# A hybrid decoder layer on one core: the gate's first block in front of the pairs, the values of heads 2 and 3 in a pair

## The chip, the cores and the metric

The kernel runs on one core of a Trainium2 chip. The metric is the device time of one execution in microseconds (us), as the median of several runs. Times within the program are us from the start of the profiled execution's span.

## The reference

The layer runs attention and a gated linear recurrence side by side on the same normalised and modulated input, and merges them by sigmoid gates. D is 1024, the sequence 1024, attention has 8 heads of 64.

```python
h = rmsnorm(x, norm_g[l]) * (1.0 + scale[:, None]) + shift[:, None]
proj = h @ w_in[l]
q_a, k_a, v_a, z_a, q_b, f_b, i_b, z_b, g_a, g_b = jnp.split(proj, cuts, axis=-1)
o_a = dilated_attention(heads_a(q_a), heads_a(k_a), heads_a(v_a), rel_bias)
o_a = o_a.reshape(B, S, ATTN_WIDTH).astype(x.dtype) * jax.nn.silu(z_a)
o_b = hgrn2_recurrence(...)   # from q_b, f_b, i_b, then rmsnorm and silu(z_b)
y = jax.nn.sigmoid(g_a) * (o_a @ w_branch_a[l]) + jax.nn.sigmoid(g_b) * (o_b @ w_branch_b[l])
x = x + gate[:, None] * (y @ w_out[l])
```

The change concerns two columns of the one large product `h @ w_in`: the values `v_a` of heads 2 and 3 (128 columns from VA + 128) and the first 128 columns of attention's gate `g_a`. The first are needed by attention, from head 2 on; the second only after attention, when its output is projected.

## The kernel before

**The stream.** The product with `w_in` is cut into blocks of 128 columns, and these are worked off as a stream of steps that fills TensorE during attention and the recurrence. Each factor is split into a high and a low part, and a product is three matmuls (L241, L242, L243). Two blocks together make a *pair* (`add_pair`), which by Strassen's scheme needs 7 steps of 12 matmuls of 512 columns; its seven products use sums of the input's quarters (b11, t1, t2, b22, b21, t3, t4). A block alone is a *unit* (`add_unit`, two steps of 24 matmuls). Of the 64 blocks, three (queries, keys and values of heads 0 and 1) are made while the input is still being prepared; 61 are left, so one unit stands in front of all pairs.

**The order.** Queries and keys of heads 2 and 3, of 4 and 5, the values of heads 4 to 7, the last queries and keys, then attention's silu inputs `z`, the gate blocks `ga`, `gb`, and the recurrence's blocks. Attention calls the stream by amounts of work (`fill`), so that a count of steps, not their contents, sets where each lies. Before a head is loaded (`load_head`), the steps that it needs are drawn forward if they are not done.

**What follows a block.** `ev_raw` copies a result to a buffer (L396) and stores it (L401). `ev_v` copies it too, but has TensorE turn it later (L452, 4 transposes for each half of the sequence), casts it into a high part on ScalarE (L456), subtracts on VectorE for the low part (L226) and stores both to `vq_d` (L458), four stores for two heads. Inside a pair, ScalarE also keeps three of the products in buffers (L330), the first of them before the product on t2 may go on in the same bank, the third before that on t3.

**The buffers.** All these results lie in one pool of six tiles of 128x512, called `ct` (`ctp`, `CT = 6`). A tile is free again when its store has landed, or when TensorE has turned it. ScalarE and VectorE work strictly in the order of their instructions, so one that waits for a free `ct` holds all behind it. Stores and weight loads leave from SP's queue, in order too; attention's own loads (L903, L909, L914) leave from GpSimd's queue.

**Around the change.** Two weight loads (w_raw6 and w_raw7) stand in SP's queue behind the last sums of the input's quarters (L685, t4), since they use that memory. Attention's first scores begin in the middle of the first pair. GpSimd waits for the last cast of the values of heads 0 and 1 (L901) before it loads the second half of head 0.

Of the kernel before, what the change touches and what calls it, by code (L numbers as in the profile page):

```python
# [19 lines left out]
P = 128  # L20
# [159 lines left out]
def hybrid_layer(ctx: ExitStack, tc: tile.TileContext, x, w_ada, b_ada, w_in, w_branch_a, w_branch_b, w_out,  # L180
# [26 lines left out]
    X = {}  # L207
# [9 lines left out]
    ga_d, gb_d, ya_d, ob_d = d8("ga_d"), d8("gb_d"), d8("ya_d"), d8("ob_d", 16)  # L217
# [5 lines left out]
    w_in_k, wba_k, wbb_k = kp(w_in), kp(w_branch_a), kp(w_branch_b)  # L223

    def sub(out_, a, hi):
        nc.vector.tensor_tensor(out_, a, hi.bitcast(F32), ALU.subtract)  # L226
# [6 lines left out]
    def banks():  # L233
        order.append(order.pop(0))
        return order[-1]

    def bank(tag):
        return pools["m"].tile([P, 512], F32, name=tag)

    def mm3(ps, ah, al, bh, bl, start, stop, more=False):  # L240
        nc.tensor.matmul(ps, ah, bh, start=start, stop=False, skip_group_check=more)  # L241
        nc.tensor.matmul(ps, al, bh, start=False, stop=False, skip_group_check=more)  # L242
        nc.tensor.matmul(ps, ah, bl, start=False, stop=stop, skip_group_check=more)  # L243

    def split(src):
        hi = wpool.tile([P, 4, P], F32R, name="w_hi")
        lo = wpool.tile([P, 4, P], F32R, name="w_lo")
        nc.scalar.copy(hi, src)  # L248
        sub(lo, src, hi)
        return hi, lo  # L250
# [6 lines left out]
    def piece(src, col, kh):  # L257
        def load(n):
            raw = raw_tile(n)
            nc.sync.dma_start(raw, src[:, 4 * kh:4 * kh + 4, col:col + P])  # L260
            return raw
        return stream.piece(load)

    def ctile(dt=F32):
        return ctp.tile([P, 512], dt, name="ct")
# [84 lines left out]
    def add_unit(src, col, rhs, ev, key=None, n=2, pre=None, alloc=None):  # L350

        stream.catch_up()
        ids = [piece(src, col, kh) for kh in range(n)]
        b = {}

        def add_half(kh):
            def prep():
                if kh == 0 and pre:
                    pre()
                parts = split(stream.tiles[ids[kh]])  # L360
                stream.done(ids[kh])
                return parts

            def run(parts):
                hi, lo = parts
                for th in range(2):
                    if th not in b:
                        b[th] = alloc() if alloc else bank(banks())
                    for k in range(4):
                        xh, xl = rhs(kh, th, k)  # L370
                        mm3(b[th], hi[:, k], lo[:, k], xh, xl, kh == 0 and k == 0, kh == n - 1 and k == 3)
                        if k < 3:
                            yield
                    if kh == n - 1:
                        ev(b[th], th, True)
                    if th == 0:
                        yield
            stream.add(prep, run)
        for kh in range(n):
            add_half(kh)  # L380
        if key:
            stream.key(key)

    QA, KA, VA, ZA = 0, AW, 2 * AW, 3 * AW
    QB, FB, IB, ZB = 4 * AW, 4 * AW + D, 4 * AW + 2 * D, 4 * AW + 3 * D
    GA, GB = 4 * AW + 4 * D, 4 * AW + 5 * D


    def half_of(th):
        return slice(512 * th, 512 * th + 512)  # L390

    def as_ct(src, psum):
        if not psum:
            return src
        t = ctile()
        nc.scalar.copy(t, src)  # L396
        return t

    def ev_raw(dst):
        def ev(src, th, psum):  # L400
            nc.sync.dma_start(dst[:, half_of(th)], as_ct(src, psum))  # L401
        return ev

    def ev_silu(dst):
        def ev(src, th, psum):
            t = ctile()
            nc.scalar.activation(t, src, AF.Sigmoid)
            out_ = t if psum else src
            nc.vector.tensor_tensor(out_, src, t, ALU.mult)
            nc.sync.dma_start(dst[:, half_of(th)], out_)  # L410
        return ev
# [9 lines left out]
    def ev_split(n, scale):  # L421
        def ev(src, th, psum):
            hi = ctile(F32R)
            if scale == 1.0:
                nc.scalar.copy(hi, src)
            else:
                nc.scalar.mul(hi, src, scale)
            lo = ctile(F32R) if psum else src.bitcast(F32R)
            if scale == 1.0:
                sub(lo, src, hi)  # L430
            else:
                nc.vector.scalar_tensor_tensor(lo, src, scale, hi.bitcast(F32), ALU.mult, ALU.subtract)
            nc.sync.dma_start(qk_d[n][:, half_of(th)], hi.bitcast(F32))
            nc.sync.dma_start(qk_d[n + 1][:, half_of(th)], lo.bitcast(F32))
        return ev

    def ev_q(p):
        return ev_split(4 * p, E ** -0.5)

    def ev_k(p):  # L440
        return ev_split(4 * p + 2, 1.0)
# [3 lines left out]
    def ev_v(p, wait=2):  # L445
        def ev(src, th, psum):
            t = as_ct(src, psum)

            def turn():
                pt = pools["t"].tile([P, 4, P], F32, name="pt")  # L450
                for n in range(4):
                    nc.tensor.transpose(pt[:, n], t[:, n * P:(n + 1) * P], ident)  # L452
                for n in (0, 2):
                    vs = ctile(F32R).rearrange("p (a h e) -> p a h e", a=2, h=2)
                    got = pt[:, n:n + 2].rearrange("p a (h e) -> p a h e", h=2)
                    nc.scalar.copy(vs[:, :, :, 0:E], got)  # L456
                    sub(vs[:, :, :, E:P], got, vs[:, :, :, 0:E])
                    nc.sync.dma_start(vq_d[p][:, 4 * th + n:4 * th + n + 2], vs.bitcast(F32))  # L458
                    last_v[p] = vs
                turned["v", p] = turned.get(("v", p), 0) + 1  # L460
            stream.after(wait, turn)
        return ev
# [28 lines left out]
    NAMES = {(0, 0): "b11", (0, 1): "b12", (1, 0): "b21", (1, 1): "b22"}  # L491
    FIRST = ((QA, ev_q(0)), (KA, ev_k(0)), (VA, ev_v(0)))
    ids = [piece(w_in_k, col, kh) for kh in range(2) for col, _ in FIRST]
    add_unit(w_in_k, VA + P, lambda kh, th, k: [t[:, k] for t in X[NAMES[kh, th]]], ev_v(1, 3), "first")
    pair = lambda a, b, ea, eb, key=None, closing=False: add_pair(w_in_k, a, b, ea, eb, key, closing)

    def pair_fq(h):
# [3 lines left out]
        pair(IB + h * P, ZB + h * P, ev_i(h), ev_silu(zb_d[h]), f"h{h}", closing)  # L501

    for p in (1, 2, 3):
        pair(QA + p * P, KA + p * P, ev_q(p), ev_k(p), f"qk{p}")
        if p == 2:
            pair(VA + 2 * P, VA + 3 * P, ev_v(2), ev_v(3), "v2")
    for m in (0, 2):
        pair(ZA + m * P, ZA + m * P + P, ev_silu(z_d[m]), ev_silu(z_d[m + 1]))
    for m in (0, 2, 4, 6):
        pair(GA + m * P, GA + m * P + P, ev_raw(ga_d[m]), ev_raw(ga_d[m + 1]))  # L510
    pair(GB, GB + P, ev_raw(gb_d[0]), ev_raw(gb_d[1]))
    pair_iz(0)
# [359 lines left out]
    with ExitStack() as at:  # L872
# [98 lines left out]
        def begin(n):  # L971

            if n < len(items):
                h, j = items[n]
                rows[n] = []
                for i in (2 * j, 2 * j + 1):
                    rows[n].append(score(h, i))
                    if i == 1:
                        if h > 0:
                            load_half(h, 1)  # L980
                        load_value(h, 1)
                    if i == 7 and h + 1 < NH:
                        load_head(h + 1)
                    yield
# [8 lines left out]
        first = begin(0)  # L993
# [510 lines left out]
```

## Time and profile before

| | us |
|---|---|
| Runs before: median (lowest to highest) | 1120.68 (1118.89 to 1120.88) |
| The profiled execution, its own time | 1119.58 |
| Its span in the profile | 1117.7 |
| TensorE busy, weight loads | 1093.9, 905.0 |
| VectorE, ScalarE, GpSimd busy | 807.4, 554.9, 124.0 |
| Start and transition, to 125 us | first pair from 83, attention's first scores at 95 |
| Attention with the stream beside it | 125 to 470 |
| Recurrence, merge and output | 470 to the end |

PE is TensorE, PEld its weight loads, DVE VectorE, ACT ScalarE, POOL GpSimd, SP the engine that issues most transfers. A row of the timeline gives start, length, engine, line, operation, what it writes from what, and in brackets the idle time ahead of it and what ended it. Where an instruction waits for several things, the bracket names the one that came last by the profile. A matmul's length is longer than its distance to the next one, because matmuls overlap. "Granted clock" is the share of TensorE's full clock that the chip allowed.

### The profile page before, as it was taken

To read this page: it belongs to the slowest core of one execution; us is meant where nothing else is said; L and a number is where in the kernel's file an instruction comes from. 1 tells how busy PE (TensorE), PEld (TensorE's weight loads), DVE (VectorE), ACT (ScalarE), POOL (GpSimd) and SP (SyncE) were. 2 spreads that over 40 slices of the span, in tenths; PEclk is the share of its full clock that TensorE was granted. 3 is DMA by queue.
4 is the path that set the end of the run, shared out by engine and by line. 5 is a ranking of instruction groups with operands and counts; after the bars stand their busy time and mean duration, and the time that the engine had idled before them with its cause. 6 is when DMAs were issued, how large, how long until landed. Compare 5 with 4: busy or idle time off the path is not lost.

```text
span 1117.7 us, 21827 instructions
## 1 busy us (share of the span) xinstructions
PE 1093.9 (98%) x8302; PEld 905.0 (81%) x8302; DVE 807.4 (72%) x1607; ACT 554.9 (50%) x1144; POOL 124.0 (11%) x207
## 2 busy tenths in 40 slices
PE   8998999999999999999999999999999999999997
PEld 6687888888888888888887888878887888888886
DVE  5586988878777776854788898897977773769053
ACT  6564656687555555632455554555554443334021
POOL 1112202203203201100000000000010012000000
PEclk9999999999999999999999999999999999999999
DMA  9849567637636624856625354453534379854052
GB/s 311 265 126 244 170 180 189 175 104 179 161 102 169 156 73 148 268 164 211 225 86 180 104 191 129 137 165 92 188 124 154 130 263 351 267 187 138 13 189 75
DMA packets 161608, 189.54 MB, mean 170 GB/s; under 512 B 11440, under 2 KB 107824, under 8 KB 161504
## 3 DMA queue, kind: packets, MB, share of 16 engines
q1 hardware_dynamic: 140080, 153.95, 43.1%
q0 software_dynamic: 21024, 33.60, 12.3%
q8 instruction: 65, 1.06, 0.4%
q10 hardware_dynamic: 400, 0.61, 0.2%
q14 instruction: 39, 0.32, 0.1%
HBM read 129.36 MB, written 58.76 MB: 168 GB/s over the span
## 4 chain that ended last, share of the span: by engine, by line
PE 79%; DVE 8%; DMA 6%; issue 3%; ACT 2%; POOL 1%; DVEq 0%; POOLq 0%; SPq 0%; ACTq 0%
PE m L241 17%; PE m L243 16%; PE m L242 16%; PE po L959 3%; PE pt L944 3%; PE pq L241 3%; PE pq L243 2%; PE pq L242 2%; PE pp L1125 2%; DMA gbr<-gb_d 2%; DVE w_lo L226 2%; PE pss L927 1%; PE pss L926 1%; DMA ld<-in_w_ada_dram 1%; PE pou L1221 1%
## 5 line engine op out<-in xcount | busy, mean ns | idle before, releaser
L226 DVE TENSOR_TENSOR w_lo<-w_raw,w_hi 128x512 fp32r<-128x512 f32 x156 | 106.9, 687 | 59.4 <-ACT w_hi L248 59.0
L248 ACT CAST w_hi<-w_raw 128x512 fp32r<-128x512 f32 x146 | 90.5, 621 | 43.7 <-PE m L243 29.2
L248 ACT CAST w_hi<-w_s 128x512 fp32r<-128x512 f32 x90 | 55.9, 621 | 56.6 <-PE m L243 37.9
L330 ACT COPY ct<-m 128x512 f32<-128x512 f32 x90 | 52.7, 585 | 58.4 <-PE m L243 48.8
L277 DVE TENSOR_TENSOR ct<-m,ct 128x512 f32<-128x512 f32 x90 | 61.8, 687 | 23.9 <-PE m L243 23.6
L226 DVE TENSOR_TENSOR w_lo<-w_s,w_hi 128x512 fp32r<-128x512 f32 x90 | 61.8, 687 | 11.7 <-ACT w_hi L248 10.6
L932 ACT ACTIVATE s<-s,st 128x128 f32<-128x128 f32 (+3 forms) x64 | 49.8, 778 | 33.0 <-DVE st L929 33.0
L948 ACT CAST pth<-pt 128x512 fp32r<-128x512 f32 (+1 forms) x80 | 43.5, 544 | 34.0 <-PE pt L944 29.7
L1229 POOL TENSOR_TENSOR ssh<-ssh,halfh 128x4 f32<-128x4 f32 x16 | 19.5, 1216 | 332.9 <-DVE ssh L1228 332.8
L226 DVE TENSOR_TENSOR ptl<-pt,pth 128x512 fp32r<-128x512 f32 (+1 forms) x80 | 50.6, 632 | 7.4 <-ACT pth L948 6.6
L241 PE MATMUL m<-t3h,w_hi 128*128 128x512 f32 x120 | 49.5, 412 | 2.2 <-ACT w_hi L248 2.2
L241 PE MATMUL m<-b22h,w_hi 128*128 128x512 f32 x124 | 50.9, 410 | 0.0
L241 PE MATMUL m<-b11h,w_hi 128*128 128x512 f32 x124 | 50.9, 410 | 0.0
L241 PE MATMUL m<-b21h,w_hi 128*128 128x512 f32 x124 | 50.6, 408 | 0.0
L241 PE MATMUL m<-t4h,w_hi 128*128 128x512 f32 x120 | 49.5, 412 | 1.1 <-issue 0.5
L242 PE MATMUL m<-b22h,w_lo 128*128 128x512 f32 x124 | 48.6, 392 | 1.8 <-issue 1.8
L241 PE MATMUL m<-t2h,w_hi 128*128 128x512 f32 x120 | 49.2, 410 | 0.7 <-ACT ct L330 0.7
L241 PE MATMUL m<-t1h,w_hi 128*128 128x512 f32 x120 | 49.4, 412 | 0.3 <-DVE ct L277 0.3
L243 PE MATMUL m<-b21l,w_hi 128*128 128x512 f32 x124 | 48.6, 392 | 0.0
L242 PE MATMUL m<-b11h,w_lo 128*128 128x512 f32 x124 | 48.6, 392 | 0.0
L243 PE MATMUL m<-b11l,w_hi 128*128 128x512 f32 x124 | 48.6, 392 | 0.0
L243 PE MATMUL m<-b22l,w_hi 128*128 128x512 f32 x124 | 48.6, 392 | 0.0
(365 smaller groups left out, 3226.6 us busy)
## 6 DMA issues: line engine op xcount, KB each, us to landing
w_raw<-in_w_in_dram SPq DMA_DIRECT2D x128, 256.0 KB, 3.5
wa<-in_w_ada_dram SPq DMA_DIRECT2D x16, 512.0 KB, 9.2
qk_d<-ct SPq DMA_DIRECT2D x32, 256.0 KB, 3.1
k<-qk_d POOLq DMA_DIRECT2D x64, 128.0 KB, 5.2
toep<-toep_d POOLq DMA_DIRECT2D x16, 256.0 KB, 5.5
qp<-qk_d POOLq DMA_DIRECT2D x32, 128.0 KB, 5.1
vq_d<-ct SPq DMA_DIRECT2D x16, 256.0 KB, 3.9
vq<-vq_d POOLq DMA_DIRECT2D x16, 256.0 KB, 4.3
```

The source lines that it names most:

```text
L226: nc.vector.tensor_tensor(out_, a, hi.bitcast(F32), ALU.subtract)
L241: nc.tensor.matmul(ps, ah, bh, start=start, stop=False, skip_group_check=more)
L242: nc.tensor.matmul(ps, al, bh, start=False, stop=False, skip_group_check=more)
L243: nc.tensor.matmul(ps, ah, bl, start=False, stop=stop, skip_group_check=more)
L248: nc.scalar.copy(hi, src)
L277: nc.vector.tensor_tensor(out_, a, b_, op)
L330: nc.scalar.copy(c[name], b[which])
L932: nc.scalar.activation(s[:, :kw], s[:, :kw], AF.Exp, bias=prev, scale=-1.0, accum_out=st2[:, 2:3])
L944: nc.tensor.transpose(pt[:, c0:c0 + P], pn[b][:, kt * P:(kt + 1) * P], ident)
L948: nc.scalar.copy(pth[:, :w], pt[:, :w])
L959: nc.tensor.matmul(po[:, 256 - n:256], vq[kt // 4][:, kt % 4], src[:, c0:c0 + n], start=kt == 0 and a == 0, stop=kt == 2 * j + 1 and a == 1)
L1125: nc.tensor.matmul(to[:, 0], k_[:, o:o + 32], q_[:, o:o + 32], start=True, stop=True)
```

## The change

The unit in front of the pairs computes the first block of `ga` instead of the values of heads 2 and 3. Those values form a new pair with the second block of `ga`, which stands behind the first pair of queries and keys. The remaining gate blocks are three pairs instead of four. The number of units, pairs, steps and matmuls is the same.

```diff
-    add_unit(w_in_k, VA + P, lambda kh, th, k: [t[:, k] for t in X[NAMES[kh, th]]], ev_v(1, 3), "first")
+    add_unit(w_in_k, GA, lambda kh, th, k: [t[:, k] for t in X[NAMES[kh, th]]], ev_raw(ga_d[0]), "first")
...
     for p in (1, 2, 3):
+        if p == 2:
+            pair(VA + P, GA + P, ev_v(1), ev_raw(ga_d[1]), "v1")
         pair(QA + p * P, KA + p * P, ev_q(p), ev_k(p), f"qk{p}")
         if p == 2:
             pair(VA + 2 * P, VA + 3 * P, ev_v(2), ev_v(3), "v2")
     for m in (0, 2):
         pair(ZA + m * P, ZA + m * P + P, ev_silu(z_d[m]), ev_silu(z_d[m + 1]))
-    for m in (0, 2, 4, 6):
+    for m in (2, 4, 6):
         pair(GA + m * P, GA + m * P + P, ev_raw(ga_d[m]), ev_raw(ga_d[m + 1]))
```

Two lines are added, so lines behind 503 have numbers higher by two in the changed kernel.

TensorE's order is the same but for the transposes of heads 2 and 3: eight in one place, between the products on t1 and t2 of the first pair, become twice four within attention. Around them other engines' orders move.

**ScalarE at the first pair.** Names carry their buffer's number here, and each row ends with what it waits for (an engine, or with DMAHW the landing of a transfer of SP's queue; eight such counters are used in turn). Before:

```order
L396 COPY ct_835<-m0_790 128x512 [waits DMAHW7_49,PE_49,Activation_49]
L396 COPY ct_849<-m1_803 128x512 [waits DMAHW0_49,PE_49,Activation_49]
L456 CAST ct_856<-pt_851 128x4x64 [waits DMAHW1_49,PE_49]
L456 CAST ct_860<-pt_851 128x4x64 [waits DMAHW4_49,DMAHW2_49,DVE_49]
L456 CAST ct_869<-pt_864 128x4x64 [waits PE_49,Activation_49]
L456 CAST ct_873<-pt_864 128x4x64 [waits DVE_49]
L248 CAST w_hi_878<-w_s_816 128x512 [waits DVE_49]
L330 COPY ct_895<-m2_882 128x512 [waits DMAHW5_49,PE_49,Activation_49]
```

In the changed kernel:

```order
L396 COPY ct_835<-m0_790 128x512 [waits DMAHW7_49,PE_49,Activation_49]
L396 COPY ct_850<-m1_803 128x512 [waits DMAHW0_49,PE_49,Activation_49]
L456 CAST ct_858<-pt_853 128x4x64 [waits DMAHW1_49,PE_49]
L456 CAST ct_862<-pt_853 128x4x64 [waits DMAHW4_49,DMAHW2_49,DVE_49]
L456 CAST ct_871<-pt_866 128x4x64 [waits DMAHW5_49,PE_49,Activation_49]
L456 CAST ct_875<-pt_866 128x4x64 [waits DVE_49]
L248 CAST w_hi_880<-w_s_816 128x512 [waits DVE_49]
L330 COPY ct_897<-m2_884 128x512 [waits PE_49]
```

The wait for the landing DMAHW5 has moved from the copy of the first product (ct_895) to the third cast of heads 0 and 1 (ct_871). The four casts of heads 2 and 3 that stood some rows further on are no longer here.

**SP's queue at the same place.** Before:

```order
L260 DMA w_raw7_976<-in_w_in_dram 128x4x128 [waits DMAHW4_49]
L458 DMA vq_d_97<-ct_856 128x512 [waits DMAHW5_49,DVE_49]
L458 DMA vq_d_97<-ct_860 128x512 [waits DMAHW6_49,DVE_49]
L458 DMA vq_d_97<-ct_869 128x512 [waits DMAHW7_49,DVE_49]
L458 DMA vq_d_97<-ct_873 128x512 [waits DMAHW0_49,DVE_49]
L458 DMA vq_d_97<-ct_922 128x512 [waits DMAHW1_49,DVE_49]
```

In the changed kernel:

```order
L260 DMA w_raw7_952<-in_w_in_dram 128x4x128 [waits DMAHW4_49]
L401 DMA ga_d_90<-ct_835 128x512 [waits DMAHW5_49,Activation_49]
L401 DMA ga_d_90<-ct_850 128x512 [waits DMAHW6_49,Activation_49]
L458 DMA vq_d_97<-ct_858 128x512 [waits DMAHW7_49,DVE_49]
L458 DMA vq_d_97<-ct_862 128x512 [waits DMAHW0_49,DVE_49]
L458 DMA vq_d_97<-ct_871 128x512 [waits DMAHW1_49,DVE_49]
```

A transfer waits for the earlier use of its own counter and then counts on it, so the landing DMAHW5 of the rows above is that of the first vq_d store before, and that of the first ga_d store (from ct_835) now.

**ScalarE where the silu inputs meet attention's exponentials.** Each change between sigmoid (L407) and exponential (L932, in the changed kernel L934) loads a table. Before:

```order
L932 ACT_TABLE_LOAD
L932 ACTIVATE s_2678,st_2679<-s_2678,st_2679 128x640
L407 ACT_TABLE_LOAD
L407 ACTIVATE ct<-ct 128x512
L932 ACT_TABLE_LOAD
L932 ACTIVATE s_2713,st_2714<-s_2713,st_2714 128x768
L964 COPY t_2730<-po_1000 64x256
L948 CAST pth<-pt 128x384
L407 ACT_TABLE_LOAD
L407 ACTIVATE ct<-ct 128x512
```

In the changed kernel, from the score of 768 columns of the same head:

```order
L934 ACT_TABLE_LOAD
L934 ACTIVATE s_2703,st_2704<-s_2703,st_2704 128x768
L407 ACT_TABLE_LOAD
L407 ACTIVATE ct<-ct 128x512
L950 CAST pth<-pt 128x512
L248 CAST w_hi<-w_raw_2119 128x512
L248 CAST w_hi<-w_s 128x512
L934 ACT_TABLE_LOAD
L934 ACTIVATE s_2775,st_2776<-s_2775,st_2776 128x896
L407 ACT_TABLE_LOAD
L407 ACTIVATE ct<-ct 128x512
L934 ACT_TABLE_LOAD
```

The sigmoids of the z blocks fall between other scores. Over the whole program there are 13 table loads on ScalarE before and 17 in the changed kernel; two of each stand at the start.

## The prediction

> **What bounds the kernel now.** I read the sums of busy time by stretch first (start and end; busy time of PE, its weight loads, VectorE, ScalarE and GpSimd, each with its count; granted clock; DMA share; GB/s).
>
> ```profile
> 90.00:103.00 13.00, 10.05 (x49) 7.93 (x47) 6.23 (x14) 4.86 (x12) 5.24 (x9) 1.00 1.23 282
> 103.00:125.00 22.00, 21.34 (x104) 16.94 (x104) 20.11 (x50) 13.88 (x31) 1.08 (x2) 1.00 0.65 191
> 125.00:470.00 345.00, 344.15 (x1835) 290.71 (x1834) 273.25 (x620) 208.61 (x411) 71.67 (x125) 1.00 0.59 159
> 470.00:1117.70 647.70, 634.31 (x5812) 524.03 (x5811) 449.96 (x823) 272.88 (x606) 33.70 (x43) 1.00 0.50 164
> ```
>
> TensorE sets the pace. Attention (125 to 470) leaves it 345.00 − 344.15 = 0.85 us idle, so nothing can be won there. The hole is at 90 to 103: 13.00 − 10.05 = 2.95 us idle, exactly where the first pair runs and where the change cuts. Next I read that place in TensorE's order of time (start, length, what, and in brackets the idle time ahead and who ended it).
>
> ```profile
> 89.81 1.04 PE L452 MATMUL pt<-kc,ct 128*128 128x128 f32 x8
> 91.56 0.50 PE L241 MATMUL m<-t2h,w_hi 128*128 128x512 f32 x1 [0.71 <-ACT ct L330]
> 100.18 0.39 PE L243 MATMUL m<-b21l,w_hi 128*128 128x512 f32 x1
> 102.81 0.49 PE L241 MATMUL m<-t3h,w_hi 128*128 128x512 f32 x1 [2.24 <-ACT w_hi L248]
> 103.53 0.50 PE L242 MATMUL m<-t3h,w_lo 128*128 128x512 f32 x1 [0.23 <-DVE w_lo L226]
> 103.87 0.40 PE L243 MATMUL m<-t3l,w_hi 128*128 128x512 f32 x1
> ```
>
> The transposes at 89.81 are those of heads 2 and 3. Then the product on t2 starts late by 0.71, and the one on t3 by 2.24 and 0.23: 3.18 us in all. ScalarE tells why.
>
> ```profile
> 84.00 1.07 ACT L396 COPY ct<-m 128x512 f32<-128x512 f32 x2
> 87.52 0.37 ACT L456 CAST ct<-pt 128x256 fp32r<-128x256 f32 x1 [0.55 <-DVE ct L226]
> 88.98 0.62 ACT L248 CAST w_hi<-w_s 128x512 fp32r<-128x512 f32 x1 [1.09 <-DVE w_s L277]
> 90.92 0.59 ACT L330 COPY ct<-m 128x512 f32<-128x512 f32 x1 [1.32 <-PE pt L452]
> 91.40 0.62 ACT L248 CAST w_hi<-w_s 128x512 fp32r<-128x512 f32 x1
> 91.92 0.59 ACT L330 COPY ct<-m 128x512 f32<-128x512 f32 x1
> 101.65 0.59 ACT L330 COPY ct<-m 128x512 f32<-128x512 f32 x1 [4.90 <-DMA vq_d<-ct]
> ```
>
> The copy at 101.65 waited 4.90 us for a ct buffer whose vq_d store had not landed; the weights of t3 stand behind it on ScalarE. There are six ct buffers, and the eight vq_d stores hold most of them. The copy at 90.92 waits for the first of these stores too: its row names TensorE, whose transposes end at 90.85, but the order's wait (DMAHW5) is a landing, and 87.06 plus 3.8 is 90.86:
>
> ```profile
> 86.02 0.94 SPq L260 DMA_DIRECT2D w_raw<-in_w_in_dram  x2
> 87.06 9.97 SPq L458 DMA_DIRECT2D vq_d<-ct  x8
> vq_d<-ct SPq DMA_DIRECT2D x2, 256.0 KB, 3.8
> vq_d<-ct SPq DMA_DIRECT2D x4, 256.0 KB, 6.8
> qk_d<-ct SPq DMA_DIRECT2D x8, 256.0 KB, 2.1
> ```
>
> (Median time from issue to landing: of the two vq_d stores issued from 87 to 88, of the four after 93.5, and of the qk_d stores at 72 to 79.)
>
> **The change, part by part.** *Removed at 89.81 to 103:* eight transposes, four casts, four subtractions, four vq_d stores. The 4.90 wait goes: the copy that waited now takes a buffer whose store was issued more than 8 us before. So t3's 2.24 and 0.23 go.
>
> *Added in the same place:* two ga_d stores. SP issues them behind the same two weight loads, which wait for the last block of x (until 84.73 + 1.22 = 85.95), so the first gate store is issued at 87.06 although its copy is done near 84.6, and it takes the place of the first vq_d store. The new point: by the order, the third cast of heads 0 and 1 (ct_871) takes the buffer of that gate store and waits for its landing, where before it ran at once. I take the same landing as for the store in that place before, so the cast starts at 90.92. ScalarE and VectorE both work in order, and behind this cast stands everything that t2 needs.
>
> ```profile
> 84.73 1.22 DVE L226 TENSOR_TENSOR t4l<-xt,t4h 128x1024 fp32r<-128x1024 f32 x1
> 87.92 0.42 DVE L226 TENSOR_TENSOR ct<-pt,ct 128x256 fp32r<-128x256 f32 x1 [0.44 <-ACT ct L456]
> 88.27 0.68 DVE L277 TENSOR_TENSOR w_s<-w_s,w_raw 128x512 f32<-128x512 f32 x1
> 89.63 0.69 DVE L226 TENSOR_TENSOR w_lo<-w_s,w_hi 128x512 fp32r<-128x512 f32 x1 [0.69 <-ACT w_hi L248]
> ```
>
> Step by step, with the distances that these rows show: cast 90.92; its subtraction 0.40 later (87.52 to 87.92), 91.32, done after 0.42 at 91.74; fourth cast 91.77, subtraction 92.17; the sum w_s 0.35 later (87.92 to 88.27), 92.52; its high part 0.71 later (88.27 to 88.98), 93.23; the copy of the first product 0.52 later (91.40 to 91.92), 93.75; t2's first matmul 0.64 later (90.92 to 91.56), 94.39. The low part is done by 93.23 + 0.65 + 0.69 = 94.57, in time for the second matmul. TensorE, without the transposes, could start t2 at 89.81, so the new hole is 4.58 us long.
>
> From t2 to the last b21 matmul it takes 100.18 − 91.56 = 8.62, which brings that one to 103.01. Nothing in between waits: t2's twelve matmuls cover the weights of the next block, and the third copy needs only t2's end. t3 then starts 0.23 later without its waits, and its third matmul stands at 103.70, where before it stood at 103.87. That is −0.17. But by then the eight transposes have not been done; they come later, in attention, at the full price of the row below, 0.89. Sum of the place: **+0.72**. What this edit wins at t3 it pays at t2.
>
> ```profile
> 89.97 0.89 PE pt L452 x8
> 114.13 0.55 PE L944 MATMUL pt<-kc,s 128*128 128x128 f32 x3 [0.35 <-DVE s L934]
> 117.94 0.39 PE L926 MATMUL pss<-k,qp 128*128 128x512 f32 x1
> 118.17 0.40 PE L927 MATMUL pss<-k,qp 128*128 128x512 f32 x1
> 118.65 0.38 PE L926 MATMUL pss<-k,qp 128*128 128x256 f32 x1
> PE po L959 <- DVE oa L965: 0.5, 1, 0.5
> 242.63 1.28 ACT L407 ACT_TABLE_LOAD   x1
> ```
>
> *The start of attention.* VectorE comes out of the 4.90 wait with a backlog (20.11 busy of 22.00), and TensorE waits 0.35 at 114.13, and 0.25 at 118.65 (matmuls of 512 columns start 0.23 apart, so it was due at 118.40). In the changed kernel VectorE works through this while t2 and b22 run, so I drop both: **−0.60** (bounds 0 and −0.60).
>
> *Heads 2 and 3 inside attention.* The transposes are in the sum. Eight casts and subtractions of 0.37 and 0.42 lie under TensorE: VectorE is busy 273.25 and ScalarE 208.61 of 345.00 there. The pacing knows only the count of steps, which is the same in both. Head 2 is loaded when 23 steps are done; its pair ends with step 18 and its values are turned two products after each result, so no step is drawn forward. The pairs of heads 4 to 7 come 7 steps later than before, heads 4 and 5 with their values at step 32 for a load at step 43. Nothing.
>
> *Sigmoid between exponentials.* The z pairs come one pair later and meet other scores: 15 table loads stand in attention's and the gates' order after the start, where 11 stood. Four times 1.28 is 5.1 us of ScalarE. In all of 125 to 440 TensorE's only wait is 0.5 us (the po row), just behind such a group at 242.63. I count one more such wait, **+0.5**; bounds 0 and, if all of it were exposed, 5.1.
>
> Without more, the profiled execution would go from 1119.58 to 1119.58 + 0.72 − 0.60 + 0.50 = 1120.2.
>
> *The clock.* A hole of this length has a second price, which the start of this trace shows.
>
> ```profile
> 20.45:23.86 3.41, 2.15 (x9) 0.98 (x9) 2.36 (x7) 2.71 (x5) 0.00 (x0) 1.00 1.02 406
> 23.86:27.28 3.42, 3.42 (x8) 2.31 (x9) 3.38 (x6) 3.36 (x6) 0.00 (x0) 0.50 1.07 360
> 98.95:102.37 3.42, 1.61 (x8) 0.99 (x6) 0.00 (x0) 0.72 (x2) 0.00 (x0) 1.00 1.27 358
> 22.45 0.50 PE L672 MATMUL pm<-b11h,w_hi 128*128 128x512 f32 x1 [0.69 <-ACT b11h L659]
> 22.79 0.40 PE L673 MATMUL pm<-b11h,w_lo 128*128 128x512 f32 x1
> 25.83 0.63 PE L672 MATMUL pm<-b11h,w_hi 128*128 128x512 f32 x1
> 26.26 0.63 PE L673 MATMUL pm<-b11h,w_lo 128*128 128x512 f32 x1
> ```
>
> A stretch of 3.41 us in which only about 0.84 us were full-size matmuls (22.45 to 23.19, and a tenth at its end) is followed by one at clock 0.50, where matmuls start 0.43 apart, not 0.23: 3.41 × (1 − 0.23/0.43) = 1.6 us lost. The stretch with 1.61 us of full-size matmuls is not followed by one. So the limit lies between 0.84 and 1.61. The present hole before t3 is about 2.4 long and leaves at least 1.0 in any stretch of 3.41. The new one is about 4.4 long (from about 90.0, where the matmul ahead ends, to 94.39): however the stretches fall, one of them holds at most 1.2 us of work, and in two thirds of the positions less than 0.84. If they went on from 23.86 in steps of 3.41, one would be 92.13 to 95.54, with 1.15 of work, and the next, all matmuls, would run at half speed. I take **+1.6**.
>
> The Trainium skill speaks against the change here, and a little differently: "TensorE: Matmul & The Clock Gate", Part 1 and the section on HAM oscillation, asks for an idle window of about 3.4 us and advises against gaps longer than that. With a wholly idle window a 4.4 us hole would trip it in some 29% of positions only; by that the sum would mostly stay at 1120.2. The trace disagrees as to the idle part: the stretch before 23.86 was not idle and still cost the clock. The row decides.
>
> Sum: 1120.2 + 1.6 = **1121.8**. The profiled execution before lay at 1119.58, 1.1 below the median of the runs, 1120.68; I don't add this, since a slow stretch more or less in the other runs may be just that difference. Against the median it is +0.1%, and below 0.2% (2.2 us) two times of this kernel can't be told apart. So I forecast no measurable change.
>
> **Rivals.**
> 1. *The clock holds* in the new hole: 1120.2, no change. For it: the 1.15 us lie between the two limits. Against: two thirds of the positions lie below both. (It is also where the rule of the Trainium skill's page "TensorE: Matmul & The Clock Gate" leads in most positions.)
> 2. *The first gate store lands late, and it is slower.* Place: the cast ct_871. If it lands after 6.8 us, like the four stores after 93.5, all behind the cast moves by 3.0: 1124.8. Beyond 3.8 + 1.1 = 4.9 us it is measurably slower. Against: those four shared the queues with GpSimd's loads, which in the changed kernel start only after the fourth cast.
> 3. *The store lands early, and it is faster.* With 2.1 us, as the qk_d stores had, the cast starts at 89.2, t2 1.7 earlier at 92.7, and the hole of 2.7 no longer takes the clock: 1120.2 − 1.7 = 1118.5. Against: two weight loads are issued right ahead of it, and the first store in this place needed 3.8.
> 4. *The table loads show*: half of the 5.1 beyond what I count gives 1121.8 + 2.1 = 1123.9, slower. Against: five such groups cost TensorE 0.5 before.
> 5. *The stores don't move the wait at all*, and the 4.90 us turn up again at the third copy: 1121.8 + 2.5 = 1124.3. The order speaks against it: that copy's buffer was stored before.
>
> **How the numbers follow.** Forecast 0.55; rival 1 0.20; rival 2 0.09; rival 3 0.07; rival 4 0.07; rival 5 0.02. Range: the forecast and rival 1 with about 1.2 to each side of them, 1119.0 to 1123.4, which leaves out most of rivals 2, 4 and 5 and of 3. Slower by over 0.2% (from 1122.9): rivals 2, 4 and 5, and a tenth of the forecast, 0.24. Faster by over 0.2% (below 1118.4): half of rival 3 and a little of rival 1, 0.07. The rest, 0.69, is no change.
>
> **What would show it.** Right: no 4.90 wait on a vq_d store at the third copy; instead ScalarE idle about 4 us ahead of a cast L456, ended by a ga_d landing at about 90.9; t2 at 94.4 with one long hole ahead of it; t3 without a wait at about 103; a stretch of granted clock 0.50 between 92 and 99. Wrong: t2 at 92 or earlier, or after 96; a wait at t3; holes in TensorE past 125 of more than 2 us together; values of head 2 waited for.

## The result, and the profile after

The change made the kernel slower, by half a percent. The forecast was no measurable change.

| | before | changed |
|---|---|---|
| Median of the runs | 1119.79 us | 1125.46 us |
| Lowest to highest, 4 runs each | 1116.81 to 1120.88 | 1124.64 to 1127.03 |
| Ratio, with 95% interval | | 1.0055 (1.0039 to 1.0070) |
| The profiled execution | 1119.58 | 1124.64 |
| Its span | 1117.7 | 1122.8 |

The same four stretches of the changed kernel, in the view of busy time by stretch (start and end; length; busy time of TensorE, its weight loads, VectorE, ScalarE and GpSimd, each with its count; granted clock; DMA share; GB/s):

```profile
90.00:103.00 13.00, 9.28 (x35) 7.53 (x36) 9.43 (x21) 6.92 (x16) 6.98 (x14) 0.87 1.13 244
103.00:125.00 22.00, 22.00 (x111) 18.48 (x110) 18.16 (x43) 12.14 (x26) 1.08 (x2) 1.00 0.64 182
125.00:470.00 345.00, 339.84 (x1812) 286.77 (x1812) 269.57 (x615) 209.58 (x407) 71.37 (x125) 1.00 0.57 155
470.00:1122.80 652.80, 641.13 (x5842) 529.48 (x5840) 454.10 (x830) 278.72 (x617) 33.65 (x43) 1.00 0.51 165
```

The first row is the predicted hole: 3.72 us idle and a mean clock of 0.87. The second row has no idle time left, where 0.66 us were idle before. The surprise is the third: attention now leaves TensorE 5.16 us idle, where it left 0.85. The list of TensorE's waits from 125 to 470 names them in one line (in all, how many, longest):

```profile
PE po L961 <- DVE oa L967: 4.8, 2, 3.7
```

TensorE's order of time gives the places of all the holes:

```profile
93.72 0.50 PE L241 MATMUL m<-t2h,w_hi 128*128 128x512 f32 x1 [4.19 <-ACT ct L330]
...
104.16 0.39 PE L241 MATMUL m<-t3h,w_hi 128*128 128x512 f32 x1
...
260.67 0.39 PE L961 MATMUL po<-pth,vq 128*128 128x256 f32 x1 [3.69 <-DVE oa L967]
...
262.98 0.63 PE L242 MATMUL m<-t1h,w_lo 128*128 128x512 f32 x1
...
305.12 0.38 PE L961 MATMUL po<-pth,vq 128*128 128x256 f32 x1 [1.16 <-DVE oa L967]
```

Around the transition ScalarE and SP's queue show the chain that was forecast: the third cast waits for the landing of a gate store.

```profile
86.64 0.91 SPq L401 DMA_DIRECT2D ga_d<-ct  x2
...
90.24 0.37 ACT L456 CAST ct<-pt 128x256 fp32r<-128x256 f32 x1 [3.97 <-DMA ga_d<-ct]
```

What stops attention stands in ScalarE's order before 260. First the kernel before, then the changed one, then VectorE in the changed one:

```profile
253.57 1.28 ACT L932 ACT_TABLE_LOAD   x1
254.86 1.04 ACT L932 ACTIVATE s<-s,st 128x896 f32<-128x896 f32 x1
...
256.02 0.37 ACT L964 COPY t<-po 64x256 f32<-64x256 f32 x1
...
257.38 1.17 ACT L932 ACTIVATE s<-s,st 128x1024 f32<-128x1024 f32 x1
```

```profile
253.67 1.05 ACT L934 ACTIVATE s<-s,st 128x896 f32<-128x896 f32 x1
...
254.83 1.28 ACT L407 ACT_TABLE_LOAD   x1
256.12 0.63 ACT L407 ACTIVATE ct<-ct 128x512 f32<-128x512 f32 x1
256.77 1.28 ACT L934 ACT_TABLE_LOAD   x1
258.07 1.15 ACT L934 ACTIVATE s<-s,st 128x1024 f32<-128x1024 f32 x1
...
259.33 0.37 ACT L966 COPY t<-po 64x256 f32<-64x256 f32 x1
```

```profile
259.54 0.75 DVE L936 TENSOR_SCALAR s<-s,st 128x1024 f32<-128x1024 f32 x1
260.21 0.41 DVE L967 TENSOR_TENSOR oa<-po,t 64x256 f32<-64x256 f32 x1
```

TensorE's next product with the values (po) needs a bank that is free only when the copy t<-po and the sum oa have read it. Before, the copy stood right behind the exponential of 896 columns. Now a table load, a Sigmoid, a second load and the exponential of 1024 columns stand between, 254.83 to 259.33, or 4.5 us. TensorE would have been ready at 256.98 (its last matmul ahead starts at 256.58 and lasts 0.40), and waits until 260.67.

Behind this hole the clock falls, as it does behind the first:

```profile
91.31:94.72 3.41, 1.00 (x4) 0.86 (x5) 2.40 (x4) 1.32 (x4) 2.88 (x8) 1.00 0.48 174
94.72:98.14 3.42, 3.42 (x9) 2.64 (x9) 2.79 (x5) 1.57 (x3) 2.88 (x6) 0.50 1.06 230
258.56:261.98 3.42, 1.31 (x8) 1.13 (x9) 2.47 (x5) 2.71 (x6) 2.12 (x4) 1.00 1.07 252
261.98:265.39 3.41, 3.41 (x12) 2.83 (x11) 1.91 (x4) 0.52 (x2) 0.00 (x0) 0.50 0.80 207
```

To see where time is lost, I compared the start of each matmul with the start of the same matmul in the profile of the kernel before, and set the difference to zero at 72 us. The columns are places of the kernel before, in us; a number that grows from one column to the next is time lost between them. All runs are listed.

| run | 104 | 125 | 240 | 254 | 306 | 469 | 1109 |
|---|---|---|---|---|---|---|---|
| changed kernel | 1.15 | 0.10 | 0.85 | 0.21 | 7.81 | 7.63 | 5.58 |
| e12, changed kernel again | 1.24 | 0.19 | 0.98 | 0.31 | 8.08 | 8.18 | 7.12 |
| e1, z back | 1.00 | −0.05 | 0.70 | 0.70 | 0.69 | 0.52 | −1.01 |
| e2, before with z later | −1.50 | −1.50 | −1.55 | −2.18 | 5.43 | 5.25 | 3.22 |
| e3, copy ahead | 0.76 | −0.23 | 0.19 | 0.69 | 2.97 | 2.80 | 1.21 |
| e4, gate store by GpSimd | −4.11 | −5.15 | −4.37 | −5.00 | 2.59 | 3.44 | 3.60 |
| e5, e1 and e4 | −4.26 | −5.25 | −4.51 | −4.51 | −4.55 | −3.70 | −4.13 |
| e6, hole filled | −0.61 | −1.59 | −0.79 | −0.79 | −0.79 | −0.21 | −1.03 |
| e7, exponential | 1.83 | 0.77 | 1.53 | 7.21 | 30.15 | 29.97 | 28.21 |
| e8, e5 and exponential | −4.29 | −5.35 | 1.19 | 7.45 | 11.43 | 11.31 | 12.39 |
| e9, tanh | 1.83 | 0.84 | 1.59 | 0.60 | 0.62 | 0.46 | −1.17 |
| e10, e5 and tanh | −4.30 | −5.29 | −4.50 | −5.49 | −5.49 | −4.89 | −6.73 |
| e11, before with tanh | −0.23 | −0.22 | −0.25 | −1.24 | −1.23 | −0.61 | −1.31 |

In the changed kernel little is lost up to 254; 7.6 us go between 254 and 306, and little after that. The 7.6 are made up of the hole at 260 (3.85), the slow stretch behind it (1.52), the hole at 305 (1.33) and smaller delays (0.85). The hole at 305 has the same form as that at 260: two table loads, a Sigmoid and the exponentials of 896 and 1024 columns stand from 297.85 on ahead of the copy at 303.77. Up to 254 two things nearly cancel: the transposes that were moved cost 0.75 by 240 (0.10 to 0.85), and 0.64 comes back between 240 and 254, where the kernel before waits 0.47 at 248.29 behind the table loads of its own z blocks, and the changed kernel, whose z blocks come later, does not.

Past 469 single profiles differ by up to 2 us either way in short holes which the profile puts down to nothing ("issue"), so the last column is only as good as that. One of these holes, 1.75 us at 843.09, lies in the profile of the kernel before and takes 0.8 to 1.9 off every row but those of e4 and e8. The profiled executions of e1, e2 and e3 are the shortest of their runs, 2.7 to 3.6 us under the medians given below.

### The profile page after: what moved, and what is told of

It reads as the page before. It is cut to its first block, busy times and chain, and to the rows that moved or that the text cites. A ratio compares the mean times of both kernels' runs of the same rounds, so it can differ in the third digit from the quotient of the medians.

```text
span 1122.8 us, 21839 instructions
## 1 busy us (share of the span) xinstructions
PE 1095.6 (98%) x8302; PEld 906.8 (81%) x8302; DVE 807.4 (72%) x1607; ACT 560.9 (50%) x1148; POOL 123.6 (11%) x207
## 4 chain that ended last, share of the span: by engine, by line
PE 90%; DVE 4%; ACT 2%; issue 2%; POOL 1%; DMA 0%; SPq 0%; POOLq 0%; DVEq 0%; ACTq 0%
PE m L241 18%; PE m L243 17%; PE m L242 17%; PE pq L241 5%; PE pq L242 5%; PE pq L243 5%; PE po L961 3%; PE pt L946 3%; PE pp L1127 2%; PE pss L929 1%; PE pss L928 1%; PE pou L1223 1%; PE pou L1208 1%; PE pou L1225 1%; PE pm L674 1%
## 5 line engine op out<-in xcount | busy, mean ns | idle before, releaser
L934 ACT ACTIVATE s<-s,st 128x128 f32<-128x128 f32 (+3 forms) x64 | 49.8, 778 | 24.7 <-DVE st L931 24.5
```

The costliest lines, as they stand in the source:

```text
L934: nc.scalar.activation(s[:, :kw], s[:, :kw], AF.Exp, bias=prev, scale=-1.0, accum_out=st2[:, 2:3])
```

## The experiments

My theory T was that the loss lies where Sigmoid's table loads stand between exponentials. Its rival C was that the hole and the slow stretch at the transition are the loss, since they had come out as forecast. Each run was timed beside the kernel before on the same chip; the ratios are to that.

**e1: the z pairs back at their old place.**

```diff
+        if p == 3:
+            for m in (0, 2):
+                pair(ZA + m * P, ZA + m * P + P, ev_silu(z_d[m]), ev_silu(z_d[m + 1]))
         pair(QA + p * P, KA + p * P, ev_q(p), ev_k(p), f"qk{p}")
...
-    for m in (0, 2):
-        pair(ZA + m * P, ZA + m * P + P, ev_silu(z_d[m]), ev_silu(z_d[m + 1]))
```

> The changed kernel with the two z pairs put ahead of the queries and keys of heads 6 and 7, so that their steps are again the 29th to 42nd of the pairs, as before the change. The unit, the pair of the values and with them the transition at 90 to 103 us stay as changed. Theory T (the time is lost where Sigmoid table loads stand between exponentials, at 254 to 305): the order of ScalarE there is again that of the kernel before, 13 table loads for 17, no wait of 3.7 us ahead of po at about 260 and no slow clock stretch behind it; 1119 to 1121 us. Rival C (the hole of 4.2 us at the transition and the slow clock stretch behind it are the loss): nothing changes, 1124.5 to 1126.

Measured: 1121.62 us beside 1120.24, ratio 1.0016 (1.0002 to 1.0031). TensorE's waits are those of the transition and the old 0.5 us:

```profile
PE m L241 <- ACT ct L330: 4.1, 1, 4.1
PE po L962 <- DVE oa L968: 0.5, 1, 0.5
```

In ScalarE's order of time the copy stands again right behind the exponential of 896 columns:

```profile
255.65 1.04 ACT L935 ACTIVATE s<-s,st 128x896 f32<-128x896 f32 x1
...
256.81 0.37 ACT L967 COPY t<-po 64x256 f32<-64x256 f32 x1
...
258.16 1.16 ACT L935 ACTIVATE s<-s,st 128x1024 f32<-128x1024 f32 x1
```

The median is 0.6 us above the expected 1119 to 1121, and the loss between 254 and 306 is gone (0.70 to 0.69). The hole and the slow stretch of the transition are still there. T holds and C falls.

**e2: the kernel before with the z pairs later.** The mirror of e1.

```diff
+    pair(GA, GA + P, ev_raw(ga_d[0]), ev_raw(ga_d[1]))
     for m in (0, 2):
         pair(ZA + m * P, ZA + m * P + P, ev_silu(z_d[m]), ev_silu(z_d[m + 1]))
-    for m in (0, 2, 4, 6):
+    for m in (2, 4, 6):
```

> The kernel before with one thing changed: the first pair of gate blocks stands ahead of the two z pairs, which thus come one pair (7 steps) later, as in the changed kernel. The unit in front is still the values of heads 2 and 3, and the transition is that of the kernel before. Theory T: ScalarE's order at the z pairs is that of the changed kernel, 17 table loads, a wait of about 3.7 us ahead of po near 260, a slow clock stretch if that hole falls so; slower by 4 to 6 us, 1123.5 to 1126. Rival C: 1119 to 1121, no difference from the kernel before.

Measured: 1126.13 beside 1120.24, ratio 1.0056 (1.0038 to 1.0075), as much as the whole change, with the old unit and the old transition. The long wait is that of the changed kernel, beside the old one at t3, which came out shorter in this execution (0.7 for 2.24, hence the −1.50 at 104):

```profile
PE po L960 <- DVE oa L966: 4.8, 2, 3.7
...
PE m L241 <- ACT w_hi L248: 0.7, 1, 0.7
```

And so is the clock, by stretches:

```profile
255.53:258.94 3.41, 0.34 (x2) 0.34 (x3) 2.14 (x5) 3.35 (x7) 2.94 (x6) 1.00 1.19 242
258.94:262.35 3.41, 3.41 (x13) 2.81 (x12) 2.55 (x5) 0.79 (x2) 0.00 (x0) 0.50 1.16 288
```

Its loss from 254 to 306 is 7.6 us (−2.18 to 5.43), the same as in the changed kernel, and it wins the same 0.64 between 240 and 254 (−1.55 to −2.18). So the place of the z pairs alone makes the loss, 7.0 us net.

**e3: the copy ahead of the loads.** The changed kernel, with the two instructions given priority.

```diff
-                nc.scalar.copy(t1, po[E:2 * E])
-                nc.vector.tensor_tensor(oa, po[0:E], t1, ALU.add)
+                with tc.high_priority():
+                    nc.scalar.copy(t1, po[E:2 * E])
+                    nc.vector.tensor_tensor(oa, po[0:E], t1, ALU.add)
```

> The changed kernel with the copy of the second half of po to t and the sum that follows it given priority in the order, so that on ScalarE the copy stands ahead of the table loads and the exponential of 1024 columns, behind the one of 896. The 17 table loads stay. Theory T in the form that the queue is what costs (the copy behind load, Sigmoid, load and exponential): the wait of 3.7 us at po near 260 falls below 1, and with it the slow clock stretch; 1119.5 to 1121.5. Its rival L (ScalarE's added 5.1 us of loads cost wherever they stand, since its other work comes later too): the wait turns up on another instruction, 1124 to 1126. Rival C: 1124.5 to 1126.

Measured: 1123.28 beside 1120.24, ratio 1.0030 (1.0014 to 1.0046), about half of the loss. ScalarE still has 17 table loads, and the copy now stands ahead of two of them:

```profile
255.57 0.37 ACT L967 COPY t<-po 64x256 f32<-64x256 f32 x1
255.96 1.28 ACT L407 ACT_TABLE_LOAD   x1
```

In the list of waits the 3.7 us have become three others:

```profile
PE pt L946 <- DVE s L936: 1.3, 1, 1.3
PE po L961 <- DVE ptl L226: 0.6, 1, 0.6
PE po L961 <- ACT pth L950: 0.5, 1, 0.5
```

Both forms are partly right. The copy's place in the queue made the one long hole, and no slow stretch follows the shorter ones. But the scores and the parts of the transposed scores come late behind the same loads, so 2.3 of the 7.6 us (0.69 to 2.97) are still lost between 254 and 306.

**e4: the gate's stores by another queue.** The changed kernel; `nc.gpsimd` issues the two stores of the first gate block.

```diff
-    def ev_raw(dst):
+    def ev_raw(dst, queue=None):
         def ev(src, th, psum):
-            nc.sync.dma_start(dst[:, half_of(th)], as_ct(src, psum))
+            (queue or nc.sync).dma_start(dst[:, half_of(th)], as_ct(src, psum))
...
-    add_unit(..., ev_raw(ga_d[0]), "first")
+    add_unit(..., ev_raw(ga_d[0], nc.gpsimd), "first")
```

> The changed kernel with one thing changed: the two stores of the first gate block leave from GpSimd's queue and not from SP's, where they stand behind two weight loads that wait for the last sums of x. They can go at about 85 and no cast of the values waits for them. If the chain of the prediction holds (cast, subtraction, sum, high part, copy, t2), t2 starts about 3 us earlier than in the changed kernel, with a hole of 1 to 2 us in place of 4.2, and no stretch of clock 0.50 behind it: 3.0 + 1.6 faster than the changed kernel, about 1121. The loss at 254 to 305 stays. Rival (another thing of the transition sets t2, or work that is drawn forward there is waited for later): 1124 to 1126.

Measured: 1122.43 beside 1120.24, ratio 1.0027 (1.0012 to 1.0043). GpSimd's and TensorE's order of time, and then the stretch of the transition:

```profile
84.41 0.58 POOL L401 DMA_DIRECT2D ga_d<-ct  x1 [3.50 <-ACT ct L396]
...
89.68 0.50 PE L241 MATMUL m<-t2h,w_hi 128*128 128x512 f32 x1 [0.20 <-ACT ct L330]
```

```profile
90.00:103.00 13.00, 12.93 (x61) 10.48 (x61) 11.48 (x25) 7.96 (x16) 4.80 (x8) 1.00 1.40 314
```

The first store goes at 84.41, where in the changed kernel it went at 86.64, and t2 starts 4.0 us earlier, not 3.0: the third cast took a buffer for which it waited for no landing. The hole is 0.20 and there is no slow stretch. At 125 the run is 5.25 us ahead of the changed kernel (0.10 to −5.15; 4.6 expected). The runs show 1.0055 − 1.0027, or 3.1 us of it, with intervals of 1.7 on each. Of the lead 0.85 is given back ahead of 469, where two products wait 0.75 and 0.32 for a VectorE sum that the changed kernel, 4 us later, doesn't wait for; the rest lies past 469, where the causes are not shown. The loss from 254 to 306 is unchanged, 7.6.

**e5: both corrections**, the edits of e1 and e4.

> The changed kernel with both corrections: the z pairs at their old place (as e1_z_back) and the first gate block's stores from GpSimd's queue (as e4_gpsimd_store). If the two losses are independent, each correction gives what it gave alone: against the changed kernel's 1125.5 that is 3.8 (e1) and 3.0 (e4), 1118.7, faster than the kernel before by about 0.15%. By the trace of e4, whose t2 came 4.0 earlier and whose transition ended 5.1 ahead, it would be up to 2 less, 1116.5. If they overlap (the recurrence gives back what comes early): 1120 to 1122.

Measured: 1115.57 beside 1119.30, ratio 0.9965 (0.9951 to 0.9979): faster than the kernel before by 0.35%, and below the 1118.7 of the simple sum. Against e1 the stores' queue is worth 0.0051, or 5.7 us, with intervals of 1.6 on each, near the 5.2 of the trace at 125 (−0.05 to −5.25).

**e6: the hole filled.** e1 with twelve matmuls that nobody reads between t1 and t2.

```diff
+                if p == 0 and th == 1:
+                    stream.after(2, fill_hole)
...
+        def fill_hole():
+            bh = X["b11"][0]
+            for _ in range(2):
+                du = pools["t"].tile([P, 4, P], F32, name="pt").rearrange("p a b -> p (a b)")
+                for n in range(6):
+                    nc.tensor.matmul(du, bh[:, 0, 0:P], bh[:, n % 4], start=n == 0, stop=n == 5)
```

> e1_z_back with twelve added matmuls of 512 columns (two sixes, of b11 with itself, into two transpose banks that are free then, read by nobody) between the products on t1 and t2, in the hole of TensorE; about 2.8 us of work in a hole of 4.1. t2 starts when it did (94.1), since ScalarE and VectorE do what they did. If the slow stretch is the answer to too little work in the stretch before it, there is no clock of 0.50 behind t2 any more, the matmuls there are 0.23 apart, and the last b22 matmul comes about 1.6 earlier; e1's 1121.6 becomes 1120. Rival (the slow stretch has another cause, or follows any first wait of this kind): 0.50 again, 1121.6. Rival (the twelve hold up t2): t2 later than 94.4.

Measured: 1119.19 beside 1119.30, ratio 1.0004 (0.9988 to 1.0020), against 1.0016 for e1. TensorE's order of time, with the twelve at L470, and two stretches:

```profile
89.40 1.52 PE L470 MATMUL pt<-b11h 128*128 128x512 f32 x6
91.94 1.63 PE L470 MATMUL pt<-b11h 128*128 128x512 f32 x6 [1.02 <-DVE ct L226]
93.59 0.50 PE L241 MATMUL m<-t2h,w_hi 128*128 128x512 f32 x1
```

```profile
89.48:92.89 3.41, 2.39 (x11) 1.71 (x10) 1.45 (x3) 1.21 (x3) 1.19 (x5) 1.00 0.85 311
92.89:96.31 3.42, 3.41 (x15) 2.47 (x15) 2.47 (x4) 2.27 (x5) 3.42 (x7) 1.00 0.61 156
```

t2 starts as late as before, the clock stays at 1.00, and by 104 the run is 1.61 us ahead of e1 (1.00 to −0.61), which is the 1.6 that the prediction put on the slow stretch. The ratios differ by 1.3 us, within their intervals, so the runs alone don't show the gain. By the trace the added work costs nothing and keeps the clock.

**e7: the sigmoid of z from the exponential.**

```diff
+            nc.scalar.activation(t, src, AF.Exp, scale=-1.0)
+            nc.vector.tensor_scalar(t, t, 1.0, None, ALU.add)
+            nc.vector.reciprocal(t, t)
-            nc.scalar.activation(t, src, AF.Sigmoid)
```

> The changed kernel with the sigmoid of z made from the exponential: ScalarE computes exp(-z), VectorE adds 1 and takes the reciprocal (two more instructions of 512 columns for each of the eight halves), the rest as before. The z pairs stay one pair later and the transition as changed, but no table is loaded in attention: 3 loads where the changed kernel has 17. Theory T: the wait of 3.7 at 260, the 1.3 at 305 and the slow clock stretch of 262 go: 1119 to 1121. Rival (the place of the z pairs costs by something else, such as the buffers that they hold, or VectorE pays for the added work): 1123 to 1126.

Measured: 1148.52 beside 1119.30, ratio 1.0253 (1.0223 to 1.0282), far outside. VectorE's groups (count, then busy time and mean ns of one), a row of its order of time and the longest of TensorE's waits say why:

```profile
L418 DVE RECIPROCAL ct<-ct 128x512 f32<-128x512 f32 x8 | 26.7, 3343 | 0.0
```

```profile
247.14 0.42 DVE L417 TENSOR_SCALAR ct<-ct 128x512 f32<-128x512 f32 x1
```

```profile
PE pss L939 <- DVE st L942: 9.2, 3, 7.1
```

A reciprocal of 512 columns takes 3.34 us, eight times the 0.42 of the addition at 247.14, and TensorE waits for what stands behind it on VectorE. The run says nothing on T.

**e8: e5 with the same edit.**

> e5_both with the sigmoid of z made from the exponential as well. What the table loads at the old place still cost (one wait of 0.5 us at po in the trace of the kernel before) goes: 0.5 under e5_both, which these rounds can hardly tell from nothing; more would mean that the loads cost TensorE in ways that the waits don't show.

Measured: 1133.60 beside 1119.30, ratio 1.0131 (1.0105 to 1.0156), the same failure, with the z pairs at their old place; nothing can be told of the 0.5.

**e9: the sigmoid of z as 0.5 + 0.5 tanh(z/2).** The changed kernel.

```diff
+            nc.scalar.activation(t, src, AF.Tanh, scale=0.5)
+            nc.vector.scalar_tensor_tensor(out_, t, 1.0, src, ALU.add, ALU.mult)
-            nc.scalar.activation(t, src, AF.Sigmoid)
-            nc.vector.tensor_tensor(out_, src, t, ALU.mult)
...
-                nc.vector.tensor_tensor(o, o, z, ALU.mult)
+                nc.vector.scalar_tensor_tensor(o, o, 0.5, z, ALU.mult, ALU.mult)
```

> The changed kernel with the sigmoid of z written as 0.5 + 0.5 tanh(z/2). The order shows no table load between this tanh and the exponentials, 3 loads in all for 17. VectorE forms (t + 1) z in the one instruction that formed t z, and the factor 0.5 goes into the product with attention's output, which is one instruction as before; no instruction is added. This is what e7_exp_sigmoid was meant to be, without the reciprocals of 3.3 us. The z pairs stay one pair later, the transition as changed. Theory T: no wait at 257 to 261 nor at 305 and no slow clock stretch there; 5 to 6 us faster than the changed kernel, 1119 to 1120.5, as e1_z_back. Rival (the later place of the z pairs costs by something other than loads): 1123 to 1126.

Measured: 1118.30 beside 1118.32, ratio 0.9989 (0.9973 to 1.0005), and 8.9 us under the changed kernel on the same chip (e12), more than the expected 5 to 6. Attention leaves TensorE 0.18 us idle, and ScalarE does 12.5 us less there than in the changed kernel:

```profile
125.00:470.00 345.00, 344.82 (x1847) 292.00 (x1845) 272.62 (x623) 197.10 (x404) 71.17 (x125) 1.00 0.59 160
```

The z pairs stand as late as in the changed kernel and nothing is lost between 254 and 306 (0.60 to 0.62). So it is the table loads, with the order that they bring, and not the later place as such: without them the copy t<-po (255.23) stands ahead of the exponential of 1024 columns (257.55) again, so this run takes away the loads and the copy's bad place together. e3 moves the copy alone, and wins back 5.3 of the 7.6. The 1.83 at 104 is the transition's: there the clock stayed at 0.50 for two stretches, from 91.92 to 98.75. The Trainium skill has the reason in "ScalarE: Activation LUTs", section "Table sets": exp and tanh are in one set, so going from one to the other loads nothing; here 3 loads are left of 17, and the trace agrees.

**e10: e5 with tanh.**

> e5_both (z pairs at the old place, the gate block's stores from GpSimd) with the tanh of e9_tanh. The 0.5 us wait at po that e5 still has goes: 1115 against e5's 1115.6, too little to tell. More than 1.5 us would mean that the loads at the old place cost TensorE more than its waits show.

Measured: 1113.70 beside 1118.32, ratio 0.9944 (0.9924 to 0.9965). This is the best version: 0.56% under the kernel before, and 1.2% (13.5 us) under the changed one in e12. Against e5 it is 0.0021, or 2.3 us, more than the 0.5 of the wait; the intervals allow from nothing to 5.

**e11: the kernel before with tanh.**

> The kernel before with the tanh of e9_tanh, nothing else: what ten table loads at the old place cost. By the one wait of 0.5 us behind such a group: 0.5 faster, within 0.2% of the kernel before.

Measured: 1117.59 beside 1118.32, ratio 0.9982 (0.9965 to 1.0000). The trace shows 1.0 us won between 240 and 254 and no more (−0.25 to −1.24). The loads thus cost about 1.0 at the old place, twice what the one named wait shows. Whether the rest of e10's 2.3 is more than scatter stays open.

**e12: the changed kernel again.**

> The changed kernel itself once more, beside the others on one chip, so that the experiments can be set against it there. 1124 to 1126, 5 to 6 us above the kernel before.

Measured: 1127.18 beside 1118.32, ratio 1.0064 (1.0038 to 1.0089). Its profile has the same two holes, 4.3 and 3.7 us, and slow stretches at 95.21 and 262.46. The interval takes in the first result.

## Why the prediction was wrong

*The stores and the new wait (right).* The first gate store took 3.50 us from issue to landing (86.64 to 90.14), with 3.8 taken from the store in its place before. The cast that was named waited for it, t2 came at 93.72 (forecast 94.39; the whole run is 0.42 earlier from its start on), and no wait stands at t3. Rivals 2, 3 and 5 fall with this. In e4, where the cast waits for no landing, 0.20 is left of the hole of 4.19.

*The clock (right, and more certain than given).* The stretch ahead held 1.00 us of work and the next ran at 0.50; e6 shows that filling it keeps the clock and wins 1.6. Rival 1 is out: all five runs with this hole and the late gate store behind SP's weight loads (e1, e3, e7, e9, e12) show a slow stretch there, as does the first profile. The share of the grid's positions with less than 0.84 us of work, given as two thirds, is 78% by the lengths that the prediction uses (3.41 and 4.4). By the rule of the Trainium skill ("TensorE: Matmul & The Clock Gate", Part 1 and the section on HAM oscillation), which asks for an idle window, only some would have. In e1 and e3 the stretch ahead was wholly idle; in the first profile and in e12 it held 1.00 and 0.95 us of work and was followed by a slow one all the same. The measurement decides: the window need not be idle.

*The transition and the transposes (about right, the transition a little too dear).* The forecast for 125 us was 0.72 − 0.89 (transposes still to come) + 1.6 − 0.60 = 0.83; measured 0.10 and 0.19, −0.05 in e1, and 0.84 in e9 with its two slow stretches. I had taken 0.60 for what comes back at the start of attention; from 104 to 125 it was 1.05 (1.15 to 0.10). The transposes, priced at 0.89, cost 0.75 to 0.79 by 240 in the changed kernel, e12, e1 and e9. So up to attention's end the change without its loss costs 0.5 to 0.7 (e1), no gain, and the 1.0016 of e1 says the same at the edge of what can be told.

*Sigmoid between exponentials (this step failed).* I counted **+0.5**, with 0 and 5.1 as bounds, because five such groups in the kernel before had cost one wait of 0.5. It measured 7.6 between 254 and 306. Against that the old wait went, which I had left in the sum: 0.64 came back between 240 and 254, so the step as a whole cost 7.0. The count was right: four more table loads, 5.1 us. Three things were wrong:

1. The price was taken from an average over groups, not from what stands in the queue. A load matters to TensorE only through an instruction behind it that TensorE waits for. In the kernel before, the copy t<-po stood ahead of the pile; in the changed kernel it stood behind two loads, a Sigmoid and the longest exponential, 4.5 us. The rows of the order that I quoted to show the loads end just short of that exponential and the copy.
2. The upper bound was not one. What an in-order queue adds to a waiting instruction is all that stands ahead of it, the 1.15 us exponential too. Hence 3.85 in one place, from two loads of 2.6 together.
3. I priced the clock for the hole that I had forecast, and not for one that my own bound allowed. The second slow stretch added 1.52.

Rival 4 named the mechanism and gave it a chance of 0.07, at 1123.9; it had the same two faults. "Holes in TensorE past 125 of more than 2 us together" was the sign named beforehand that the prediction is wrong, and it is what the profile shows: 4.8.

*The balance of the profiled execution.* Forecast 1121.80, measured 1124.64, so 2.84 too little: +6.46 for the Sigmoid step (6.96 for 0.5), −0.73 at the transition, −0.14 for the transposes, −0.18 from 306 to 469, −2.05 from 469 to 1109, −0.10 behind that and −0.42 at the start. The parts past 469 and at the start have no cause that the profile shows; 1.40 of the 2.05 lies at the hole of 843.09 in the profile before. So it is luck that the profiled execution came as near; the median, 1125.46, lies 3.7 above the forecast.

## What to carry to other kernels

Where a planner moves work of one kind past work of another, look up what stands behind each insertion in the in-order queues, find the instruction that the bounding engine waits for (here a small copy that frees a bank), and add up all that is ahead of it; an average price from the profile before is no price for a new order. Two functions that share an engine but not a table are best brought into one set: here tanh for Sigmoid beside Exp removed the loss at either place, with no added instruction. A store whose buffer is wanted soon should not queue behind loads that wait for something else, and a hole that can't be closed can at least be filled so that the clock holds.

## What was not expected of the hardware

**Where the clock falls.** In one execution the slow stretches begin on a fixed grid: in the changed kernel at 23.04, 94.72 and 261.98, which are 71.68 and 167.26 apart, 21.0 and 49.0 times 3.413 us. The grid lies differently in each execution. Of all stretches on the grid that ran at full clock, the one with the most work that was followed by a slow one is of e7:

```profile
264.35:267.76 3.41, 1.44 (x7) 0.82 (x5) 3.41 (x3) 1.17 (x2) 3.15 (x6) 1.00 0.98 248
267.77:271.18 3.41, 2.13 (x7) 1.91 (x8) 3.38 (x9) 1.86 (x3) 1.10 (x2) 0.50 0.70 199
```

The one with the least work that was not followed by a slow one is the first of these of e12; the second was:

```profile
88.38:91.79 3.41, 1.60 (x8) 0.98 (x6) 0.42 (x1) 0.52 (x2) 0.00 (x0) 1.00 1.04 372
91.79:95.21 3.42, 0.95 (x4) 0.81 (x5) 2.41 (x4) 1.33 (x4) 2.84 (x8) 1.00 0.46 168
95.21:98.62 3.41, 3.41 (x10) 2.63 (x9) 2.73 (x5) 1.61 (x3) 3.40 (x6) 0.50 1.05 236
```

In all profiles, between 60 and 1100 us, the limit thus lies between 1.44 and 1.60 us of TensorE busy in 3.41, about 42 to 47%, where I had it between 0.84 and 1.61. By that, a hole of 4 us between full-size matmuls leaves a stretch below the limit however the grid falls (at least 2.0 idle in one of two), and one of less than 1.8 us in none. Ahead of 60 us the limit doesn't hold: there stretches with up to 2.24 us busy were followed by a slow one. In the prediction's row at 20.45 it is 2.15, of which about 0.84 are full-size matmuls and the rest smaller products; how such products are counted is not shown.

**A slow reciprocal.** VectorE's reciprocal of 128x512 takes 3.34 us, and its other instructions on that size in these runs 0.36 to 0.81.
